# Local attention in windows of 64: transfers of 512 rows instead of 256, four q and k rows per partition, and small extra loads

## The chip, the core and the metric

The kernel runs on one NeuronCore of a Trainium2 chip. The metric is the device time of one execution, in microseconds, and lower is better. A profile shows one execution; its span is about 1.9 us shorter than the device time.

Three words are used throughout. A *transfer* is one DMA instruction. It is cut into *packets*, each on one of the core's 16 *DMA engines*. An engine that has finished its share of a transfer reports it, so each transfer has 16 *landings* (the records of the kernel before hold 4,240 for 265 transfers), and it is complete at the last.

## The reference, cut to what matters

```python
B, S, D, W = 4, 4096, 1536, 64          # q, k, v: float32, 16,384 rows of 1,536
logits = einsum('bnwd,bnud->bnwu', q_w, k_w) * D**-0.5    # windows of 64 rows
attn   = exp(logits - max); attn = attn / attn.sum(-1)
out    = einsum('bnwu,bnud->bnwd', attn, v_w)
```

Each row of q, k and v is read once and each row of the output is written once. Nothing is shared between windows.

## The kernel before

The 16,384 rows are cut into 63 units of 256 rows (R = 2 rows per partition) and 2 last units of 128 rows. Loads convert float32 to fp16 on the way and are issued by Pool, three units ahead. Stores are issued by Pool too; only the three stores of the last unit come from SP.

```python
AHEAD = 3
inp  = tile_pool(bufs=AHEAD + 1)      # q, k, v: [128, 2, 1536] fp16
outp = tile_pool(bufs=4)              # output:  [128, 2, 1536] fp32
def dram(x, u):                       # two adjacent rows per partition
    return x[u.row0 : u.row0 + u.rows].rearrange("(p r) d -> p (r d)", p=P, r=u.R)

def transpose(src, xt, c0, copy):     # PE transposes into PSUM, then one copy to SBUF
    ...
    copy(out=xt[:, c0 : c0 + CG, :R, :], in_=tp)          # contiguous
def scores(u): ...                    # q, k transposed; k q^T; exp into a block-diagonal tile
def values(u, et, last):
    u.o = outp.tile([P, RM, D], FP32)                     # waits for a free output buffer
    ...                               # et^T v, scaled by 1/sum, by ScalarE and VectorE in turn
    if last: nc.sync.dma_start(...)   # three 128x512 stores

for i, u in enumerate(units):
    if i + AHEAD < N: load_all(units[i + AHEAD])          # 3 transfers
    et = scores(u); values(u, et, i == N - 1)
    if i == N - 8: ...                # this one store is cut into four transfers
    elif i < N - 1: store(u)          # 1 transfer
```

The softmax here doesn't subtract the row's maximum and nothing guards it: scores larger than these inputs give would overflow.

## Time and profile before

| | before |
|---|---|
| device time | 953.67 us (952.92 to 954.0, 3 runs) |
| HBM traffic | 302 MB read, 101 MB written |
| DMA, mean share of the span | full in 39 of 40 slices |
| PE, DVE, ACT busy | 66%, 38%, 31% |
| last landing, end of span | 950.8 us, 952.2 us |

These are lines of the page of the kernel before. The DMA row holds the busy share of the 16 engines in 40 slices of the span, in tenths, with 9 for 90% or more. The queue lines hold packets, MB, and packet time as a share of 16 engines' span. The COPY lines hold the count, the busy time and the mean ns of one copy, and then the engine's idle time before it.

```profile
span 952.2 us, 13234 instructions
...
PE 629.0 (66%) x5624; PEld 430.1 (45%) x5624; DVE 363.6 (38%) x584; ACT 291.0 (31%) x515; POOL 139.8 (15%) x267
...
DMA  9999999999999999999999999999999999999997
...
DMA packets 37868, 252.53 MB, mean 265 GB/s; under 512 B 4264, under 2 KB 4264, under 8 KB 29752
...
q0 software_dynamic: 37376, 250.89, 101.9%
q8 instruction: 44, 0.72, 0.3%
...
L131 DVE COPY xk<-tp 128x1024 f16<-128x1024 f16 (+1 forms) x128 | 88.2, 689 | 253.4 <-PE tp L130 253.4
...
L131 ACT COPY xk<-tp 128x1024 f16<-128x1024 f16 (+1 forms) x65 | 65.4, 1006 | 354.3 <-PE tp L130 354.3
```

The DMA engines are full from start to end and no compute engine is. The list of waits says the same from the other side. Its columns are the waiting engine and line, what it waited for, total us, times, and the longest wait:

```profile
engine line waited for: us in total, times, longest us
...
POOL k L82 <- DMA k<-in_k_dram: 180.3, 58, 4.0
...
PE tp L130 <- DMA k<-in_k_dram: 127.1, 63, 3.0
...
PE tp L130 <- DMA q<-in_q_dram: 59.6, 48, 8.1
```

PE waits for loads. Pool waits as well: it issues a transfer every 3.66 us, a transfer lands 28.8 us after its issue, so about eight are under way, and Pool issues the next only when an older one is done.

The packet records add the price of a packet. Packets that carry 12,288 bytes of HBM traffic start 455 ns apart on one engine, and packets of 6,144 bytes 229 ns apart. Twice the bytes cost 226 ns more, so about 3 ns belong to the packet itself; 6,144 bytes in 226 ns are 27.2 bytes per ns and engine. (To a tenth, from the distances of packets one to four places apart on an engine: 229.3 and 455.2 ns, and 907.0 ns for the packets of 24,576 bytes of the changed kernel. Either doubling leaves 3.4 ns for the packet, so the 3.5 ns used below agrees with the trace.) It is the HBM side that counts here: a load writes only 6,144 bytes of fp16 into SBUF, a store reads 12,288 bytes from it, and yet their packets are spaced alike, 455 and 456 ns. The 474 ns that the trace records for one load packet are no measure of its price, as a packet overlaps the next.

### The profile page before, as it was taken

The numbers are of one execution on the slowest core, as the hardware profiler recorded it, in microseconds if no ns is written. First come the engines' busy times: TensorE is split into PE (matmuls) and PEld (weight loads), VectorE is DVE, ScalarE is ACT, GpSimd is POOL, SyncE is SP. The second block draws the span as 40 slices with busy tenths as digits, with TensorE's granted clock in tenths as the row PEclk, the third lists the DMA queues.
The fourth block names the chain that finished last, engine by engine and source line by source line (L and its number), as shares of the span: only waits on it lengthen the run. The fifth ranks groups of instructions, "written<-read, shape, count | busy, mean of one in ns | idle before, by whom it ended". The sixth has DMA issues, their size and how long they took to land. (4 is left out here: it accounts for less than half of the span.)

```text
span 952.2 us, 13234 instructions
## 1 busy us (share of the span) xinstructions
PE 629.0 (66%) x5624; PEld 430.1 (45%) x5624; DVE 363.6 (38%) x584; ACT 291.0 (31%) x515; POOL 139.8 (15%) x267
## 2 busy tenths in 40 slices
PE   5766666676757666766666676756766667667663
PEld 3544344454445444444444454444443445444442
DVE  3434434334343342433433334334333343443432
ACT  2432332323323233233232323322323233233232
POOL 3111111111111111111111111111111111111210
PEclk9989998989998998999999889899999898999896
DMA  9999999999999999999999999999999999999997
GB/s 185 209 280 274 255 281 255 273 277 251 281 267 262 280 254 275 273 257 281 263 266 279 256 275 268 261 281 262 267 273 262 275 265 263 277 265 268 270 279 263
DMA packets 37868, 252.53 MB, mean 265 GB/s; under 512 B 4264, under 2 KB 4264, under 8 KB 29752
## 3 DMA queue, kind: packets, MB, share of 16 engines
q0 software_dynamic: 37376, 250.89, 101.9%
q8 instruction: 44, 0.72, 0.3%
q1 hardware_dynamic: 432, 0.79, 0.2%
q14 instruction: 16, 0.13, 0.0%
HBM read 301.99 MB, written 100.66 MB: 423 GB/s over the span
## 5 line engine op out<-in xcount | busy, mean ns | idle before, releaser
L136 PE MATMUL lt<-xq,xk 128*128 128x256 f16 (+1 forms) x1536 | 228.9, 305 | 19.8 <-DVE xk L131 19.4
L130 PE MATMUL tp<-ident,k 128*128 128x128 f16 x1536 | 132.1, 247 | 128.1 <-DMA k<-in_k_dram 127.1
L136 PEld LDWEIGHTS <-xk 128*128 128x128 f16 x1536 | 154.8, 109 | 69.3 <-DVE xk L131 40.9
L131 DVE COPY xk<-tp 128x1024 f16<-128x1024 f16 (+1 forms) x128 | 88.2, 689 | 253.4 <-PE tp L130 253.4
L180 PE MATMUL o<-v,et 128*128 128x512 f16 x762 | 184.2, 378 | 0.0
L130 PEld LDWEIGHTS <-k 128*128 128x128 f16 x1536 | 113.8, 113 | 144.6 <-DMA k<-in_k_dram 139.3
L131 ACT COPY xk<-tp 128x1024 f16<-128x1024 f16 (+1 forms) x65 | 65.4, 1006 | 354.3 <-PE tp L130 354.3
L188 DVE TENSOR_SCALAR out_sb<-o,rs 128x512 f32<-128x512 f32 x191 | 143.4, 751 | 69.0 <-PE o L180 68.9
L186 ACT ACTIVATE out_sb<-o,rs 128x512 f32<-128x512 f32 x193 | 132.6, 688 | 82.6 <-PE o L180 82.5
L159 ACT ACTIVATE et<-lt,zeros 32x128 f16<-32x128 f32 (+1 forms) x256 | 91.7, 358 | 215.7 <-PE lt L136 210.9
L131 DVE COPY xq<-tp 128x1024 f16<-128x1024 f16 (+1 forms) x193 | 121.4, 681 | 54.1 <-PE tp L130 53.2
L130 PE MATMUL tp<-ident,q 128*128 128x128 f16 x1536 | 100.7, 224 | 60.1 <-DMA q<-in_q_dram 59.6
L130 PEld LDWEIGHTS <-q 128*128 128x128 f16 x1536 | 89.5, 100 | 89.8 <-DMA q<-in_q_dram 88.6
L180 PEld LDWEIGHTS <-et 128*128 128x128 f16 x762 | 68.7, 96 | 84.4 <-issue 24.2
L173 DVE RECIPROCAL rs<-sp 128x2 f32<-128x2 f32 (+1 forms) x65 | 11.1, 171 | 203.0 <-PE sp L168 203.0
L168 PE MATMUL sp<-ones,et 128*128 128x1 f16 x254 | 16.2, 167 | 106.5 <-ACT et L159 106.5
L168 PEld LDWEIGHTS <-et 128*128 128x128 f16 x254 | 10.6, 96 | 124.5 <-ACT et L159 124.5
L196 POOL DMA_DIRECT2D out_dram<-out_sb x65 | 34.9, 537 | 210.7 <-ACT et L159 103.9
L82 POOL DMA_DIRECT2D v<-in_v_dram x65 | 34.5, 531 | 199.0 <-DMA v<-in_v_dram 123.0
L82 POOL DMA_DIRECT2D q<-in_q_dram x65 | 34.7, 534 | 189.1 <-DMA q<-in_q_dram 145.3
L82 POOL DMA_DIRECT2D k<-in_k_dram x65 | 34.5, 531 | 189.6 <-DMA k<-in_k_dram 180.3
L207 POOL DMA_DIRECT2D out_dram<-out_sb x2 | 1.0, 510 | 6.3 <-ACT et L159 3.2
(10 smaller groups left out, 3.0 us busy)
## 6 DMA issues: line engine op xcount, KB each, us to landing
out_dram<-out_sb POOLq DMA_DIRECT2D x62, 1536.0 KB, 28.7
q<-in_q_dram POOLq DMA_DIRECT2D x63, 768.0 KB, 28.8
k<-in_k_dram POOLq DMA_DIRECT2D x63, 768.0 KB, 28.8
v<-in_v_dram POOLq DMA_DIRECT2D x63, 768.0 KB, 28.8
out_dram<-out_sb POOLq DMA_DIRECT2D x1, 1344.0 KB, 19.0
q<-in_q_dram POOLq DMA_DIRECT2D x2, 384.0 KB, 24.2
k<-in_k_dram POOLq DMA_DIRECT2D x2, 384.0 KB, 22.4
v<-in_v_dram POOLq DMA_DIRECT2D x2, 384.0 KB, 20.6
```

Of the source, the lines that this page charges most:

```text
L82: nc.gpsimd.dma_start(out=dst, in_=dram(src, u))
L130: nc.tensor.transpose(tp[:, c - c0, r, :], src[:, r, c * P : (c + 1) * P], ident)
L131: copy(out=xt[:, c0 : c0 + CG, :R, :], in_=tp)
L136: nc.tensor.matmul(lv[:, r, :, :], lhsT=xk[:, c, r, :], rhs=xq[:, c, :R, :], start=(c == 0 and r == 0), stop=(c == DC - 1), skip_group_che ...
L159: nc.scalar.activation(et[s, :, :, s], lv[s, :, :, s], EXP, bias=zeros[s], scale=scale)
L168: nc.tensor.matmul(sp[:, t, 0:1], lhsT=et[:, r, t, :], rhs=ones[:, 0:1], start=(r == 0), stop=(r == R - 1),)
L173: nc.vector.reciprocal(out=rs, in_=sp[:, :, 0])
L180: nc.tensor.matmul(o, lhsT=et[:, r, t, :], rhs=u.v[:, r, sl], start=(r == 0), stop=(r == R - 1),)
L186: nc.scalar.activation(dst, o, COPY, bias=0.0, scale=rs[:, t : t + 1])
L188: nc.vector.tensor_scalar_mul(dst, o, scalar1=rs[:, t : t + 1])
L196: nc.gpsimd.dma_start(out=dram(of, u)[a:b], in_=src[a:b])
L207: nc.gpsimd.dma_start(out=dst[:, r, :], in_=src[:, r, :])
```

## The change

The intent is to pay less per byte moved. A unit becomes 512 rows, so there are half as many transfers. q and k take four adjacent rows per partition, so their packets double to 24,576 HBM bytes. v and the output stay at two rows per partition. The attention blocks are still 256 rows, so the transposed q and k have to be re-interleaved in the copy out of PSUM. The memory for that comes from fewer buffers: two output buffers of 512 rows stand for four of 256. Two PSUM pools change as well: `lt_ps` goes from one buffer to two, `o_ps` from three to two. Fourteen tiny loads of 1 to 15 rows that nobody uses are added from unit 13 to unit 27 of 32, apparently to shift work between DMA engines, and the cut of one late store goes.

```diff
-AHEAD = 3
+AHEAD = 2
+SLOTS = 4
...
+    units = [Unit(i * UR, [(0, 4, 2)]) for i in range(N - 1)]          # UR = 512
+    units.append(Unit((N - 1) * UR, [(0, 2, 2), (2, 3, 1), (3, 4, 1)]))
...
-    xtp = ctx.enter_context(tc.tile_pool(name="xtp", bufs=2))
-    outp = ctx.enter_context(tc.tile_pool(name="outp", bufs=4))
+    xtp = ctx.enter_context(tc.tile_pool(name="xtp", bufs=1))
+    outp = ctx.enter_context(tc.tile_pool(name="outp", bufs=2))
...
+        r = R if name == "v" else hi - lo
+        dst = slots(getattr(u, name), lo, hi, r)
+        nc.gpsimd.dma_start(out=dst, in_=rows(src, u.first[i], hi - lo, r))
...
-            copy(out=xt[:, c0 : c0 + CG, :R, :], in_=tp)
+            dst = xt[:, c0 : c0 + CG, :].rearrange("p c (r e j) -> p (c r) j e", r=R, j=H)
+            copy(out=dst, in_=tp)
...
-        if i == N - 8:
-            ...                                   # one store cut into four transfers
+        n = ui - 12
+        if 1 <= n <= 15 and n != 8:
+            w = 128 + 4 * n
+            nc.gpsimd.dma_start(out=probe[:n, n, :w], in_=qf[0:n, :w])
```

ScalarE also takes 5 of 12 copies instead of 2 of 12.

More of the change, by code (lines that the diff above doesn't have):

```diff
@@ L17, with __init__ @@
 class Unit:
-    def __init__(self, row0, R):
-        self.row0, self.R = row0, R
-        self.rows = P * R
-def plan(total):
-    tail = [1, 1]
-    units, row = [], 0
-    body = total - P * sum(tail)
-    while row < body:
-        units.append(Unit(row, 2))
-        row += units[-1].rows
-    for R in tail:
-        units.append(Unit(row, R))
-        row += units[-1].rows
-    assert row == total
-    return units
-AHEAD = 3
+    def __init__(self, row0, parts):
+        self.row0, self.parts = row0, parts
+        self.first = [row0 + P * lo for lo, hi, R in parts]
+AHEAD = 2
+SLOTS = 4
 @with_exitstack
@@ L56 @@
     scale = float(D) ** -0.5
-    RM = 2
     qf, kf, vf, of = (x.rearrange("b s d -> (b s) d") for x in (q, k, v, out))
-    units = plan(B * S)
-    N = len(units)
+    UR = P * SLOTS
+    N = B * S // UR
+    units = [Unit(i * UR, [(0, 4, 2)]) for i in range(N - 1)]
+    units.append(Unit((N - 1) * UR, [(0, 2, 2), (2, 3, 1), (3, 4, 1)]))
     consts = ctx.enter_context(tc.tile_pool(name="consts", bufs=1))
     inp = ctx.enter_context(tc.tile_pool(name="inp", bufs=AHEAD + 1))
-    xtp = ctx.enter_context(tc.tile_pool(name="xtp", bufs=2))
@@ L66 @@
-    outp = ctx.enter_context(tc.tile_pool(name="outp", bufs=4))
+    xtp = ctx.enter_context(tc.tile_pool(name="xtp", bufs=1))
+    outp = ctx.enter_context(tc.tile_pool(name="outp", bufs=2))
     rsp = ctx.enter_context(tc.tile_pool(name="rsp", bufs=4))
     tp_ps = ctx.enter_context(tc.tile_pool(name="tp_ps", bufs=3, space=bass.MemoryType.PSUM))
-    lt_ps = ctx.enter_context(tc.tile_pool(name="lt_ps", bufs=1, space=bass.MemoryType.PSUM))
-    o_ps = ctx.enter_context(tc.tile_pool(name="o_ps", bufs=3, space=bass.MemoryType.PSUM))
+    lt_ps = ctx.enter_context(tc.tile_pool(name="lt_ps", bufs=2, space=bass.MemoryType.PSUM))
@@ L71, with rows, slots @@
+    o_ps = ctx.enter_context(tc.tile_pool(name="o_ps", bufs=2, space=bass.MemoryType.PSUM))
     s_ps = ctx.enter_context(tc.tile_pool(name="s_ps", bufs=1, space=bass.MemoryType.PSUM))
-    def dram(x, u):
-        return x[u.row0 : u.row0 + u.rows].rearrange("(p r) d -> p (r d)", p=P, r=u.R)
     ctx.enter_context(tc.manual_schedule())
-    def load(u, name):
+    def rows(x, row0, n, r):
+        return x[row0 : row0 + P * n].rearrange("(h p r) d -> p h (r d)", p=P, r=r)
+    def slots(t, lo, hi, r):
+        return t[:, lo:hi, :].rearrange("p (h r) d -> p h (r d)", r=r)
@@ L79, in load @@
+    def load(u, i, name):
+        lo, hi, R = u.parts[i]
+        if not hasattr(u, name):
+            setattr(u, name, inp.tile([P, SLOTS, D], FP16, tag=name + "16", name=name + "16"))
         src = {"q": qf, "k": kf, "v": vf}[name]
-        t = inp.tile([P, RM, D], FP16, tag=name + "16", name=name + "16")
-        dst = t[:, : u.R, :].rearrange("p r d -> p (r d)")
-        nc.gpsimd.dma_start(out=dst, in_=dram(src, u))
-        setattr(u, name, t)
+        r = R if name == "v" else hi - lo
+        dst = slots(getattr(u, name), lo, hi, r)
+        nc.gpsimd.dma_start(out=dst, in_=rows(src, u.first[i], hi - lo, r))
@@ L85, in load_all @@
     def load_all(u):
-        for name in "qkv":
-            load(u, name)
+        for i in range(len(u.parts)):
+            for name in "qkv":
+                load(u, i, name)
     load_all(units[0])
@@ L108 @@
     ets = {}
-    for R in sorted({u.R for u in units}):
+    for R in (2, 1):
         ets[R] = []
@@ L115, with scores, product @@
     turn = {R: 0 for R in ets}
-    def scores(u):
-        R = u.R
-        CG = 4 if R == 2 else 6
-        xq = xtp.tile([P, DC, RM, P], FP16, tag="xq", name="xq")
-        xk = xtp.tile([P, DC, RM, P], FP16, tag="xk", name="xk")
-        lt = lt_ps.tile([P, 512], FP32, tag="lt", name="lt")
-        lv = lt[:, : R * R * P].rearrange("p (r s e) -> p r s e", r=R, s=R)
+    flip = [0]
+    def scores(u, i):
+        lo, hi, R = u.parts[i]
+        n = hi - lo
+        H = n // R
+        CG = {4: 2, 2: 4, 1: 6}[n]
+        xq = xtp.tile([P, DC, n * P], FP16, tag="xq", name="xq")
+        xk = xtp.tile([P, DC, n * P], FP16, tag="xk", name="xk")
+        lts = []
+        for h in range(H):
+            lt = lt_ps.tile([P, 512], FP32, tag="lt", name="lt")
+            lts.append(lt[:, : R * R * P].rearrange("p (r s e) -> p r s e", r=R, s=R))
         def transpose(src, xt, c0, copy):
-            tp = tp_ps.tile([P, CG, R, P], FP16, tag="tp", name="tp")
+            tp = tp_ps.tile([P, CG * R, H, P], FP16, tag="tp", name="tp")
             for c in range(c0, c0 + CG):
                 for r in range(R):
-                    nc.tensor.transpose(tp[:, c - c0, r, :], src[:, r, c * P : (c + 1) * P], ident)
-            copy(out=xt[:, c0 : c0 + CG, :R, :], in_=tp)
-        def product(c0):
+                    for j in range(H):
+                        nc.tensor.transpose(
+                            tp[:, (c - c0) * R + r, j, :],
+                            src[:, lo + R * j + r, c * P : (c + 1) * P],
+                            ident,
+                        )
+            dst = xt[:, c0 : c0 + CG, :].rearrange("p c (r e j) -> p (c r) j e", r=R, j=H)
+            copy(out=dst, in_=tp)
+        def product(c0, h):
             for c in range(c0, c0 + CG):
+                kc = xk[:, c, :].rearrange("p (r h e) -> p r h e", r=R, h=H)
+                qc = xq[:, c, :].rearrange("p (r h e) -> p r h e", r=R, h=H)
                 for r in range(R):
                     nc.tensor.matmul(
-                        lv[:, r, :, :],
-                        lhsT=xk[:, c, r, :],
-                        rhs=xq[:, c, :R, :],
+                        lts[h][:, r, :, :],
+                        lhsT=kc[:, r, h, :],
+                        rhs=qc[:, :, h, :],
                         start=(c == 0 and r == 0),
@@ L146, in scores, with values @@
         for c0 in starts:
-            transpose(u.q, xq, c0, nc.vector.tensor_copy)
-        for i, c0 in enumerate(starts):
-            transpose(u.k, xk, c0, nc.scalar.copy if i == 1 else nc.vector.tensor_copy)
-            if i > 0:
-                product(starts[i - 1])
-        product(starts[-1])
-        et = ets[R][turn[R] % 2]
-        turn[R] += 1
-        n = W // R
-        for w in range(P // n):
-            s = slice(w * n, (w + 1) * n)
-            nc.scalar.activation(et[s, :, :, s], lv[s, :, :, s], EXP, bias=zeros[s], scale=scale)
-        return et
-    def values(u, et, last):
-        R = u.R
-        u.o = outp.tile([P, RM, D], FP32, tag="out_sb", name="out_sb")
+            flip[0] += 1
+            transpose(getattr(u, "q"), xq, c0, nc.scalar.copy if flip[0] % 3 == 0 else nc.vector.tensor_copy)
+        for g, c0 in enumerate(starts):
+            transpose(getattr(u, "k"), xk, c0, nc.scalar.copy if g % 2 == 1 else nc.vector.tensor_copy)
+            if g > 0:
+                for h in range(H):
+                    product(starts[g - 1], h)
+        blocks = []
+        for h in range(H):
+            product(starts[-1], h)
+            et = ets[R][turn[R] % 2]
+            turn[R] += 1
+            w = W // R
+            for a in range(0, P, w):
+                s = slice(a, a + w)
+                nc.scalar.activation(
+                    et[s, :, :, s], lts[h][s, :, :, s], EXP, bias=zeros[s], scale=scale
+                )
+            blocks.append((h, et))
+        return blocks
+    def values(u, i, h, et, last):
+        lo, hi, R = u.parts[i]
+        if not hasattr(u, "o"):
+            u.o = outp.tile([P, SLOTS, D], FP32, tag="out_sb", name="out_sb")
         sp = s_ps.tile([P, R, 2], FP32, tag="sp", name="sp")
@@ L180, in values @@
                     nc.tensor.matmul(
-                        o, lhsT=et[:, r, t, :], rhs=u.v[:, r, sl],
+                        o, lhsT=et[:, r, t, :], rhs=u.v[:, lo + R * h + r, sl],
                         start=(r == 0), stop=(r == R - 1),
                     )
-                dst = u.o[:, t, sl]
+                dst = u.o[:, lo + R * h + t, sl]
                 if n % 2 == 0:
@@ L190, in values, with store @@
                 if last:
-                    nc.sync.dma_start(out=of[u.row0 : u.row0 + u.rows, sl], in_=u.o[:, 0, sl])
-    def store(u, parts=((0, P),)):
-        src = u.o[:, : u.R, :].rearrange("p r d -> p (r d)")
-        for a, b in parts:
-            nc.gpsimd.dma_start(out=dram(of, u)[a:b], in_=src[a:b])
-    for i, u in enumerate(units):
-        if i + AHEAD < N:
-            load_all(units[i + AHEAD])
-        et = scores(u)
-        values(u, et, i == N - 1)
-        if i == N - 8:
-            src = u.o[0:8, : u.R, :]
-            dst = of[u.row0 : u.row0 + 8 * u.R].rearrange("(p r) d -> p r d", r=u.R)
-            for r in range(u.R):
-                nc.gpsimd.dma_start(out=dst[:, r, :], in_=src[:, r, :])
-            store(u, ((8, 16), (16, P)))
-        elif i < N - 1:
-            store(u)
+                    nc.sync.dma_start(out=of[u.first[i] : u.first[i] + P, sl], in_=dst)
+    def store(u, i):
+        lo, hi, R = u.parts[i]
+        nc.gpsimd.dma_start(out=rows(of, u.first[i], hi - lo, R), in_=slots(u.o, lo, hi, R))
+    probe = consts.tile([16, 16, 192], FP32, name="probe")
+    for ui, u in enumerate(units):
+        if ui + AHEAD < N:
+            load_all(units[ui + AHEAD])
+        n = ui - 12
+        if 1 <= n <= 15 and n != 8:
+            w = 128 + 4 * n
+            nc.gpsimd.dma_start(out=probe[:n, n, :w], in_=qf[0:n, :w])
+        for i in range(len(u.parts)):
+            last = ui == N - 1 and i == len(u.parts) - 1
+            for h, et in scores(u, i):
+                values(u, i, h, et, last)
+            if not last:
+                store(u, i)
 _INS = ['q', 'k', 'v']
```

## The prediction

> **What bounds it now: the DMA engines' data rate.** The slice table shows DMA at 9 tenths in all but the last slice; the queue table has the software queue at 101.9% of 16 engines. PE is busy 66%, DVE 38%, ACT 31%. In the list of waits PE waits for k (127 us) and q (60 us), and the Pool timeline shows one transfer issued every 3.66 us, each blocked until an older one lands: the queue is never empty. In the packet records, packets of 12,288 HBM bytes follow each other on one engine at 455 ns, those of 6,144 at 229 ns: a packet by itself costs 3 ns. The recorded 474 ns of a load packet overlaps its successor. [...] The floor: 402.65 MB are 2,048 such packets per engine, 932 us, before start, completion packets and imbalance.
>
> **The imbalance.** The 16 completion times of one transfer spread from 0.8 us at first to 9 us at the end. 44 instruction-fetch packets (16 KB, 0.9 us each) recur with period 8: eight engines carry 5 or 6 each and end 5.5 to 9 us behind. The slowest sets the end.
>
> **What the change does.**
> - q and k: one packet of 24,576 HBM bytes instead of two of 12,288; per 512 rows 16 fewer packets per engine, 16 x 3.5 ns = 0.06 us.
> - Transfers per 512 rows halve from 8 to 4. A fast engine takes 14.63 us per 256 rows; its 32 packets explain 14.56, so a boundary costs 18 ns; 4 fewer: 0.07 us. A transfer's latency (28.8 us, nearly all queueing) is already hidden.
> - Together 0.13 us of 29.28 us per 512 rows, times 31: 4 us. The removed split of one late store: 0.2 us.
> - 14 tiny loads: a completion packet per engine and few short packets, 0.4 us. They can't move work between engines, as large transfers give each engine eight partitions anyway. PE's instruction count is unchanged (11,250), so fetches and lag stay.
> - Compute: interleaved writes make DVE copies slower (0.69 to about 1.1 us, an estimate[...]); ACT takes 5 of 12 copies instead of 2. Now a unit ends 10.3 us after k lands (PE timeline); I estimate 19 us for 512 rows, 11 us after v lands. The period is 29 us and 30 us of transfers stand behind it: DMA never starves, slower copies cost nothing.
> - Tail: the last loads are followed by 20 us of stores, into which the last compute fits. Start: unchanged.
>
> **Prediction: 949.8 us, 80% range 944.5 to 954.5.** Faster by over 2% (below 935): 3%; within 2%: 94%; slower: 3%. More than 2% would have to beat the floor plus start and lag.
>
> **What would show it.** Right: DMA at 9 tenths throughout; about 29.15 us per 512 rows; q and k packets of 12,288 written bytes spaced 907 ns; final lag 8 to 10 us; DVE copies near 1.1 us without effect. Wrong: packets split again (952); a shrinking spread of landings (tiny loads do balance: up to 4 us more, as the mean lag is 4 and the slowest 9); DMA slices below 9[...].
>
> **What would make it wrong.** Long packets that delay fetches or run at another rate per byte; compute outlasting the stores at the end; tiny loads stalling an engine for their latency; contention from engines moving to other partitions.

## More of the kernel before

Times here are medians.

## The result, and the profile after

| | before | after |
|---|---|---|
| device time | 953.81 us (4 runs) | 954.15 us (953.58 to 955.36, 4 runs) |
| ratio, 95% interval | | 1.0007 [0.999, 1.0024] |
| packets in the software queue | 37,376 | 27,824 |
| DVE copy, ACT copy | 0.69, 1.01 us | 1.27, 1.29 us |
| last landing, end of span | 950.8, 952.2 us | 950.9, 951.8 us |

A ratio is the mean time of one kernel's runs over that of the other's of the same rounds, so it is not quite the ratio of the medians.

The gain of 4 us that was forecast is absent. These are the lines of the page of the changed kernel that answer to those above:

```profile
span 951.8 us, 12993 instructions
...
PE 668.1 (70%) x5624; PEld 439.5 (46%) x5624; DVE 424.8 (45%) x489; ACT 431.0 (45%) x610; POOL 91.6 (10%) x154
...
DMA  9999999999999999999999999999999999999996
...
DMA packets 28313, 252.57 MB, mean 265 GB/s; under 512 B 2545, under 2 KB 2656, under 8 KB 12256
...
q0 software_dynamic: 27824, 250.96, 100.6%
q8 instruction: 44, 0.72, 0.3%
...
L141 ACT COPY xk<-tp 128x1024 f16<-128x1024 f16 (+1 forms) x96 | 123.5, 1287 | 233.8 <-PE tp L135 233.8
...
L141 DVE COPY xk<-tp 128x1024 f16<-128x1024 f16 (+1 forms) x97 | 123.3, 1271 | 178.6 <-PE tp L135 178.6
```

The packets did get fewer, and those of q and k start 907 ns apart, as forecast. The body of the kernel did get faster too. The landings of the transfers give the time per 512 rows, taken over 24 units in the middle and averaged over the 16 engines. It is 29.406 us before; with the changed kernel it is 29.289 us, taken from the run without the tiny loads below, where equal stretches are easily counted (29.307 us with them). The difference of 0.117 us, times 31, is 3.6 us.

So the gain is earned in the body and lost elsewhere. The page's slices are 24 us wide and hide the place; shorter stretches show it. These lines of the stretch view hold, for each stretch, its length, the busy time of each engine with its instructions, the granted PE clock, the DMA share and GB/s. GB/s counts bytes as they are written, so a load, which turns float32 into fp16, counts half of its HBM traffic. This is the kernel before:

```profile
100.00:840.00 740.00, 495.32 (x4420) 338.37 (x4420) 284.94 (x452) 225.97 (x401) 106.75 (x201) 0.92 1.03 268
...
920.00:936.00 16.00, 10.12 (x86) 6.52 (x84) 5.43 (x10) 6.18 (x12) 2.14 (x4) 0.93 1.05 309
936.00:950.00 14.00, 6.04 (x40) 3.81 (x40) 2.59 (x5) 2.79 (x5) 0.00 (x0) 0.50 0.69 274
```

And these are the same stretches of the changed kernel:

```profile
100.00:840.00 740.00, 534.33 (x4462) 350.77 (x4458) 337.01 (x377) 339.23 (x477) 70.02 (x114) 0.88 1.02 270
...
920.00:936.00 16.00, 3.47 (x8) 1.05 (x8) 1.50 (x2) 2.01 (x3) 0.00 (x0) 0.52 0.90 358
936.00:950.00 14.00, 7.76 (x81) 5.45 (x79) 5.24 (x10) 6.32 (x12) 1.09 (x2) 0.87 0.59 237
```

From 920 to 936 us PE of the changed kernel does 8 matmuls instead of 86, and Pool issues nothing. From 936 to 950 us the DMA engines have too little to do, at 237 GB/s. The list of waits of the changed kernel for 905 to 952 us names the cause:

```profile
engine line waited for: us in total, times, longest us
POOL out_dram L214 <- DVE xq L141: 23.1, 1, 23.1
...
ACT out_sb L205 <- DMA out_dram<-out_sb: 14.1, 1, 14.1
DVE out_sb L207 <- DMA out_dram<-out_sb: 13.6, 1, 13.6
```

Pool's wait is put down to a DVE copy, but that is only the last semaphore of several; the first place to look is ScalarE. This is its timeline in the changed kernel (start, us, what, and in brackets the idle time before it and what ended it):

```profile
916.19 1.51 ACT L174 ACTIVATE et<-lt,zeros 32x128 f16<-32x128 f32 x4 [2.58 <-PE lt L148]
931.79 0.69 ACT L205 ACTIVATE out_sb<-o,rs 128x512 f32<-128x512 f32 x1 [14.09 <-DMA out_dram<-out_sb]
```

The last unit has its scores at 917.7 us, but it may not write its output: with two output buffers it needs the one of the unit two before, and the store of that unit, issued at 910.1 us, has landed completely only at 931.7 us, as it stood in a deep queue. After that, three small blocks of compute are left, each with its store. The queue runs dry meanwhile: the last store that was waiting in it ends on the 16 engines between 931.0 and 939.0 us, and the next one is issued at 937.6 and lands at 942.9 us.

### The profile page after: what moved, and what is told of

Its sections match the earlier page's. It is cut to its first block, busy times and chain, and to the rows that moved or that the text cites. A ratio compares the mean times of both kernels' runs of the same rounds, so it can differ in the third digit from the quotient of the medians.

```text
span 951.8 us, 12993 instructions
## 1 busy us (share of the span) xinstructions
PE 668.1 (70%) x5624; PEld 439.5 (46%) x5624; DVE 424.8 (45%) x489; ACT 431.0 (45%) x610; POOL 91.6 (10%) x154
## 3 DMA queue, kind: packets, MB, share of 16 engines
q0 software_dynamic: 27824, 250.96, 100.6%
## 4 chain that ended last, share of the span: by engine, by line
DMA 63%; PE 13%; ACT 7%; another core or an unknown queue 7%; DVE 6%; issue 2%; POOL 1%; ACTq 0%; POOLq 0%; DVEq 0%
DMA out_dram<-out_sb 47%; DMA q<-in_q_dram 9%; PE o L199 8%; DMA k<-in_k_dram 7%; PE lt L148 3%; ACT out_sb L205 3%; DVE out_sb L207 3%; PE tp L135 3%; ACT et L174 2%; ACT xk L141 2%; DVE xk L141 2%; DVE xq L141 1%; ACT xq L141 0%; POOL out_dram L214 0%
## 5 line engine op out<-in xcount | busy, mean ns | idle before, releaser
L199 PE MATMUL o<-v,et 128*128 128x512 f16 x762 | 237.6, 420 | 91.2 <-ACT out_sb L205 86.8
L141 ACT COPY xk<-tp 128x1024 f16<-128x1024 f16 (+1 forms) x96 | 123.5, 1287 | 233.8 <-PE tp L135 233.8
L141 DVE COPY xk<-tp 128x1024 f16<-128x1024 f16 (+1 forms) x97 | 123.3, 1271 | 178.6 <-PE tp L135 178.6
L199 PEld LDWEIGHTS <-et 128*128 128x128 f16 x762 | 74.0, 101 | 220.3 <-issue 183.3
L141 DVE COPY xq<-tp 128x1024 f16<-128x1024 f16 (+1 forms) x129 | 152.2, 1255 | 12.6 <-PE tp L135 12.5
L141 ACT COPY xq<-tp 128x1024 f16<-128x1024 f16 x64 | 82.1, 1283 | 91.4 <-PE tp L135 91.4
L214 POOL DMA_DIRECT2D out_dram<-out_sb x33 | 23.8, 720 | 391.2 <-DVE out_sb L207 269.9
L187 PEld LDWEIGHTS <-et 128*128 128x128 f16 x254 | 14.3, 102 | 61.8 <-ACT et L174 50.3
L79 POOL DMA_DIRECT2D v<-in_v_dram x34 | 23.6, 694 | 180.8 <-DMA out_dram<-out_sb 51.1
L79 POOL DMA_DIRECT2D q<-in_q_dram x34 | 18.6, 546 | 114.1 <-DMA probe<-in_q_dram 53.1
L79 POOL DMA_DIRECT2D k<-in_k_dram x34 | 18.6, 547 | 78.2 <-DMA k<-in_k_dram 37.2
```

The costliest lines, as they stand in the source:

```text
L79: nc.gpsimd.dma_start(out=dst, in_=rows(src, u.first[i], hi - lo, r))
L141: copy(out=dst, in_=tp)
L187: nc.tensor.matmul(sp[:, t, 0:1], lhsT=et[:, r, t, :], rhs=ones[:, 0:1], start=(r == 0), stop=(r == R - 1),)
L199: nc.tensor.matmul(o, lhsT=et[:, r, t, :], rhs=u.v[:, lo + R * h + r, sl], start=(r == 0), stop=(r == R - 1),)
L214: nc.gpsimd.dma_start(out=rows(of, u.first[i], hi - lo, R), in_=slots(u.o, lo, hi, R))
```

## The experiments

Runs sent together share a chip and the runs of the kernel before. Unless said otherwise each had five rounds, and the kernel before has 9 runs in each group.

### The changed kernel again

> The changed kernel again, as the yardstick of this chip. Every theory expects what was measured: the same time as the kernel before, ratio 0.999 to 1.002.

Measured: 953.95 us against 952.86 us, ratio 1.001 [0.9997, 1.0022]. The absence of a gain stands.

### Without the tiny loads

```diff
-        n = ui - 12
-        if 1 <= n <= 15 and n != 8:
-            ...
-            nc.gpsimd.dma_start(out=probe[:n, n, :w], in_=qf[0:n, :w])
```

> The changed kernel without its 14 tiny loads. My prediction: they cost 0.4 us and balance nothing, so 0 to 0.6 us faster than the changed kernel, and the spread of the 16 landings at the last 512-row store stays near 8 us. Rival (the tiny loads balance the DMA engines): 2 us or more slower, and the spread grows. Rival (each tiny load stalls an engine for its latency, and that ate the gain): 4 us faster.

Measured: 953.23 us, ratio to before 1.0001 [0.9987, 1.0014], 0.7 us below the changed kernel of the same chip. The interval of each ratio is wider than that difference, but all five runs (952.45 to 953.61 us) lie below all five of the changed kernel (953.70 to 954.56 us), so it is a small cost. The spread of the 16 landings of the last 512-row store is 7.8 us without them and 8.5 us with them in this group (8.0 us in the first profile of the changed kernel). They balance nothing, and they are not where 4 us went.

### With a third output buffer

The tiny loads and their tile of 12 KB per partition are left out to make room for the third output buffer. So this run is to be read against the one before it.

```diff
-    outp = ctx.enter_context(tc.tile_pool(name="outp", bufs=2))
+    outp = ctx.enter_context(tc.tile_pool(name="outp", bufs=3))     # and no tiny loads
```

> No tiny loads (that frees the memory) and three output buffers of 512 rows instead of two. Theory (the last unit cannot write its output before the store of the unit two before it has landed, so the queue runs dry at the end): the 14 us wait of ScalarE for a store near the end is gone, the queue stays full to the end, and the time falls by 4 to 5 us against the run without tiny loads, to about 949 us, ratio to the kernel before 0.995. Rival (the gain was never there, or the slower PSUM copies ate it): within 1 us of the run without tiny loads.

Measured: 951.9 us, ratio to before 0.9988 [0.9975, 1.0001]; 1.3 us below the run without tiny loads, not 4 to 5. In the trace the mechanism came out fully. The two late stretches of this run, in the same columns as above:

```profile
920.00:936.00 16.00, 8.82 (x88) 5.22 (x86) 5.90 (x12) 7.64 (x13) 1.09 (x2) 0.97 1.02 413
936.00:950.00 14.00, 0.00 (x0) 0.00 (x0) 0.00 (x0) 0.00 (x0) 0.00 (x0) 0.50 0.43 175
```

The wait is gone from ScalarE's timeline:

```profile
916.65 1.51 ACT L174 ACTIVATE et<-lt,zeros 32x128 f16<-32x128 f32 x4 [2.58 <-PE lt L148]
918.96 0.69 ACT L205 ACTIVATE out_sb<-o,rs 128x512 f32<-128x512 f32 x1 [0.80 <-PE o L199]
```

All compute is over before 936 us, DMA stays full to there, and the last landing comes at 946.8 us, against 950.5 us without the third buffer and 950.8 us in the kernel before. That is about the 4 us that the prediction promised, at the last landing. (The 3.7 us compare two runs of one chip. The profile of the kernel before is of an execution of 954.1 us, up to 1.3 us longer than that kernel's medians in the other groups, so the 4.0 us against it may hold as much too much.) But the span ends at 950.0 us, 3.2 us after it, where in the kernel before it ended 1.5 us after. The semaphore records show who was late: SP had seen its last store at 946.9 us, and Pool came to the closing barrier only at 949.3 us. Pool spends that time in the drain instruction at the end of the program.

These are end times in us after the start of the span, taken from the records of the runs (those further down included). "Pool" and "SP" are the last landing of a transfer issued by each:

```
                                 Pool    SP      Pool's drain ends   span ends
before                           949.4   950.8   951.5               952.2
changed                          947.0   950.9   950.0               951.8
no tiny loads                    946.3   950.5   948.9               951.4
third output buffer              946.6   946.8   949.2               950.0
  and last unit stored from SP   945.8   946.9   948.3               949.1
    same, two rows per partition 947.2   948.1   948.3               949.1
  and last two units from SP     945.2   947.0   947.7               948.5
  and last three units from SP   944.5   949.0   947.0               950.0
```

In each row the drain ends later than Pool's last landing, by 2.1 to 3.0 us in all but one and by 1.2 us in that one. In the changed kernel SP's last landing is later than the drain, and in the kernel before the drain outlasts it by 0.7 us only. The drain does not wait for all data, whoever issued it: in the changed kernel and in the last row it ends before SP's last landing. The third buffer brings SP's landing forward to Pool's, and the drain comes out as the last thing to end, 2.4 us after the data.

### The kernel before with two output buffers

```diff
-    outp = ctx.enter_context(tc.tile_pool(name="outp", bufs=4))
+    outp = ctx.enter_context(tc.tile_pool(name="outp", bufs=2))     # of 256 rows
```

> The kernel before with two output buffers of 256 rows instead of four. Theory of the output buffers: its last block too has to wait for a late store, so 2 to 4 us slower than the kernel before, all of it in the last 30 us, with the period per 512 rows still 29.3 us. Rival (output buffers do not matter, as compute has idle time): within 0.5 us of the kernel before.

Measured: 954.32 us, ratio 1.0014 [1.0002, 1.0027]: slower, by 1.5 us and so less than expected. The waits of this run (columns as above) show how little a wait tells by itself:

```profile
engine line waited for: us in total, times, longest us
ACT out_sb L186 <- DMA out_dram<-out_sb: 231.8, 61, 14.1
DVE out_sb L188 <- DMA out_dram<-out_sb: 201.1, 61, 13.6
```

ScalarE now waits for a store in 61 of the 65 units, 232 us in all, a line that the kernel before does not have at all. Yet the time per 512 rows is 29.404 us against 29.406. The waits cost nothing in the body, where the queue holds work for longer than they last. So the loss lies outside the body. In the profile the last landing comes at 951.3 us instead of 950.8, and the 16 landings of the last stores lie within 0.3 us, so there too the queue had run dry. The rest of the 1.5 us is not traced.

### The end, with the last unit stored from SP

```diff
+        queue = nc.sync if u is units[-1] else nc.gpsimd
-        nc.gpsimd.dma_start(out=rows(...), in_=slots(...))
+        queue.dma_start(out=rows(...), in_=slots(...))      # on top of the third buffer, no tiny loads
```

> Three output buffers, no tiny loads, and the two stores of the last unit that Pool issued are now issued from SP, so that Pool's last transfer lands some 7 us earlier. Theory (in the run with three buffers the data was done at 946.8 us but Pool reached the closing barrier only at 949.3 us, 2.7 us after its last transfer had landed; that delay ate the gain): Pool is no longer last, the span ends about 0.9 us after the last landing, near 947.7 us, and the time is 949.0 to 950.2 us, ratio to the kernel before 0.9966. Rival (the end is set by something else): as with Pool stores, 951.9 us, ratio 0.9988.

Measured: 950.79 us against 953.69 us, ratio 0.9973 [0.9961, 0.9986]. The drain theory was right in direction, but gained only about two thirds of what was expected from it (the ratio went from 0.9988 to 0.9973, where 0.9966 was expected): Pool's last transfer did not land 7 us earlier but at 945.8 us. SP's stores shared the engines with it and passed it: SP's store that was issued after Pool's last one had landed by 935.6 us, and Pool's landed by 945.8 us; from 926 to 934 us, 129 large packets of SP's queue started beside 150 of Pool's. (Together that is one per 459 ns on each of 16 engines, about the spacing of one queue alone.)

### Two rows per partition for q and k as well

This run moves the same 512 rows per transfer, but with the packets of the kernel before and contiguous copies.

```diff
-        r = R if name == "v" else hi - lo
+        r = R
-            dst = xt[:, c0 : c0 + CG, :].rearrange("p c (r e j) -> p (c r) j e", r=R, j=H)
+            dst = xt[:, c0 : c0 + CG, :].rearrange("p c (r j e) -> p (c r) j e", r=R, j=H)
```

> As the run with SP stores at the end, but q and k are loaded with two adjacent rows per partition, as v is: twice the packets for q and k, the same number of transfers, and contiguous PSUM copies. My prediction of 3.5 ns per packet: 0.06 us more per 512 rows, so 1.7 to 1.9 us slower than that run. Rival (packet size is worth nothing): equal within 0.5 us. Rival (the interleaved copies cost time): faster by 1 us or more.

Measured: 950.74 us, ratio to before 0.9971 [0.9959, 0.9984], equal to the run above, so the expectation for the time failed. In the body the expected cost is there: 29.345 us per 512 rows against 29.283 us, 0.05 to 0.06 us more by whichever transfer one follows, where 0.056 were forecast. The last landing is at 948.1 us instead of 946.9. In both runs, though, Pool's drain ended at 948.3 us, and it set the end in both (here only 1.2 us after Pool's last landing, which hides the later data; why, no run shows, so the equal times are a coincidence as far as is known). The run splits the gain of the change: of 0.12 us per 512 rows, half comes from the longer packets and half from fewer transfers. Both are as small as the 3.5 ns per packet and 18 ns per transfer of the prediction.

### The changed kernel with contiguous copies, wrong on purpose

```diff
-            dst = xt[:, c0 : c0 + CG, :].rearrange("p c (r e j) -> p (c r) j e", r=R, j=H)
+            dst = xt[:, c0 : c0 + CG, :].rearrange("p c (r j e) -> p (c r) j e", r=R, j=H)
```

The rows are then paired wrongly, and the result is wrong. This run had three rounds (4 runs).

> The changed kernel with contiguous instead of interleaved PSUM copies: rows are paired wrongly, so the result is wrong on purpose. Theory (the copies are off the path, the end waits for an output buffer): DVE copies back near 0.69 us and ScalarE copies near 1.0 us, but the time equals the changed kernel's within 0.5 us, about 954. Rival (slower copies ate the gain): 2 to 4 us faster.

Measured: 953.96 us, ratio to before 1.0007 [0.9991, 1.0022], the time of the changed kernel. Two lines of its page show that the copies did become fast:

```profile
L141 ACT COPY xk<-tp 128x1024 f16<-128x1024 f16 (+1 forms) x96 | 96.7, 1008 | 235.7 <-PE tp L135 235.7
...
L141 DVE COPY xk<-tp 128x1024 f16<-128x1024 f16 (+1 forms) x97 | 66.8, 689 | 237.4 <-PE tp L135 237.4
```

Summed over the q and k copies of both engines, the copies of the changed kernel are busy for 481 us (123.5 + 123.3 + 152.2 + 82.1) and those of this run for 311 us (96.7 + 66.8 + 82.8 + 64.5). The 170 us of additional work on two engines cost no time. The slower copies are not where the gain went.

### The kernel before with late stores from SP

```diff
+        queue = nc.sync if u in units[-3:] else nc.gpsimd
```

> The kernel before with the stores of its third- and second-last blocks issued from SP. Theory of Pool's late close: there Pool was last too, reaching the barrier at 951.5 us, 2.1 us after its last transfer landed at 949.4, against 950.9 for SP; so 0.5 to 0.9 us faster than before, no more, as the slowest DMA engine's work is the same. Rival (stores from SP are cheaper in themselves): 2 us or more faster.

Measured: 954.01 us, ratio 1.0009 [0.9996, 1.0021]. It did not get faster, so this expectation failed too. The trace shows why: SP's stores share the engines with the loads of the last unit, which stand in Pool's queue. The last load landed at 944.9 us instead of 939.7, the last unit was computed later, and SP's last store landed at 952.2 us instead of 950.8. Stores from SP are no cheaper; they only go to another place in the line.

### Two units stored from SP

```diff
-        queue = nc.sync if u is units[-1] else nc.gpsimd
+        queue = nc.sync if u in units[-2:] else nc.gpsimd
```

> As the run with SP stores at the end, but the store of the second-last 512-row unit is issued from SP as well. In that run Pool's last transfer (that very store) was overtaken by SP's and landed only at 945.8 us, and Pool's closing drain ended at 948.3 us. Theory (the drain ends 1 to 3 us after Pool's last transfer has landed): Pool's last transfer now lands before 942 us, its drain ends before 945, SP is last, the span ends 0.9 us after the last landing, near 947.8 us, and the time is 949.2 to 950.0 us, 1 us below the run before it. Rival (the drain ends when all data has been moved, whoever issued it): no change, 950.8 us.

Measured: 950.04 us against 953.18 us, ratio 0.9968 [0.9954, 0.9981]. The time is at the edge of what was expected, but the way there was not: Pool's last transfer landed at 945.2 us, not before 942, and its drain still ended last, at 947.7 us. This is the fastest version, and it beats both kernels by a third of a per cent. Its lead over the run with one unit (ratio 0.9973 [0.9961, 0.9986]) is within the noise.

### Uneven stores, to even out the engines

The tiny loads had one use: their packets have sizes of their own, so the trace shows on which engines a transfer of n partitions lands. Their start times fit one reading, that n partitions go to the same first n engines, the first four of which are early ones: from two rows on a load of n rows has n packets, and from 9 to 15 rows the first four start within 0.94 us in each load (0, 0.11, 0.46 and 0.94 us), while the rows added start later, the last of the 15 at 7.98 us.

```diff
+        cuts = [0, 112, 116, 120, 124, P] if u in units[-3:-1] else [0, P]
+        for a, b in zip(cuts, cuts[1:]):
+            queue.dma_start(out=dst[a:b], in_=src[a:b])
```

> As the run with two units stored from SP, but the 512-row stores of the third-last and second-last units are cut: 112 partitions go out evenly, and the last 16 in four transfers of four partitions each. The tiny loads of the changed kernel showed that a transfer of n partitions uses the same first n engines, and that the first four are among those without instruction fetches. Theory (lag comes from the fetches, and only an uneven split can even it out): the first four engines get 5.5 us more work, the others 1.8 us less, the spread of the last landings falls from about 8.7 us to 7 or less, and the time falls by 1.5 to 1.8 us against the run of this call without the cuts. Rival (lag is not a matter of work per engine, or the small transfers cost more than they shift): no gain, or slower.

Measured: 957.58 us, ratio 1.0045 [1.0032, 1.0059], slower by 7.5 us than the run without the cuts. The large late packets grew: 35 of those after 880 us took over 1.2 us, and none in the run without cuts.

```diff
-        cuts = [0, 112, 116, 120, 124, P] ...
+        cuts = [slice(0, 112)] + [slice(112 + a, P, 4) for a in range(4)] ...
```

> As the run with the cut stores, but each of the four-partition transfers takes every fourth of the last 16 partitions instead of four adjacent ones. There, 46 of the late large packets took over 1.2 us; in the run without cuts none did. Theory[...]: the packets over 1.2 us go down to 10 or fewer, and the time falls from 957.6 us to 949 to 952 us. Rival (the partition order does not matter; any such cut costs this much): again about 957 us.

(The 46 in this text were counted with a limit of 1.0 us; with 1.2 us it is 35.) Measured: 954.55 us, ratio 1.0008 [0.9995, 1.0022], and 15 packets over 1.2 us. Spreading the partitions took back 3 us of the 7.5 and 20 of the 35 long packets, so the order of the partitions matters. Why it does was not shown. And about half of the loss remained, and neither theory's number was met. Whether the lag of eight engines can be evened out at all is left open.

### Three units stored from SP

```diff
-        queue = nc.sync if u in units[-2:] else nc.gpsimd
+        queue = nc.sync if u in units[-3:] else nc.gpsimd
```

> As the run with two units stored from SP, but three. Theory (Pool's closing drain ends 1 to 3 us after its last transfer, and SP's transfers share the engines with Pool's): Pool's last transfer is now a load and lands before 940 us, its drain ends before 943, SP is last and the span ends 0.9 us after the last landing: 949.2 to 950.0 us, 0 to 0.8 us below the run with two units. Rival (as in the kernel before with SP stores: the loads are pushed back, and the last blocks are computed too late): 950.5 us or more.

Measured: 952.58 us, ratio 0.9993 [0.9981, 1.0006]. The rival was right: the last load landed at 944.5 us, the last output was computed at 946.8 us, and SP's last store landed at 949.0 us. So two units are better than three; from one unit they can't be told apart.

## Why the prediction was wrong

**Right: the bound.** The DMA engines' byte rate is the limit (their share is 1.03 and 1.02 from 100 to 840 us, before and after), and the floor of 932 us was not approached. Slower copies, more ScalarE work and, in the run with two output buffers, 232 us of new ScalarE waits all left the body at the same time per 512 rows.

**Right: the size of the gain in the body.** 0.13 us per 512 rows were forecast and 0.117 us measured. (The 29.28 and 29.15 us of the prediction are those of a fast engine; the earliest of the 16 went from 29.28 to 29.17 us.) The two terms were tested apart: longer packets 0.06 us (0.06 forecast), fewer transfers the rest, 0.06 us (0.07 forecast). With the third buffer, the last landing is 4.0 us earlier than in the kernel before (946.8 against 950.8 us), of which 0.2 us were forecast from the store that is no longer cut.

**Right: the tiny loads.** They move nothing; removing them gained 0.7 us, where 0.4 us had been forecast; the 0.3 us between are within the noise of the runs.

**Right in effect, off in size: the copies.** VectorE's went from 0.69 to 1.27 us, not 1.1, which was the author's estimate. The interleaved write, with a step of two elements, is what made them slower: with contiguous writes and nothing else changed, in the run that was wrong on purpose, they took 0.69 us again. That ScalarE's copies would slow down as well, from 1.01 to 1.29 us, was not foreseen. Neither cost time.

**Wrong: the tail.** The step that failed is this one: "Tail: the last loads are followed by 20 us of stores, into which the last compute fits." The count of stores was right. The compute would have fit, as the run with a third buffer shows, where all of it was over before 936 us. What was overlooked is that compute needs a place to write. The prediction costed packets, transfers and copies, but passed over one line of the diff, four output buffers becoming two. They hold the same bytes, so it looked neutral. But a buffer is released only when the whole store from it has landed, so what counts is how late in the queue that store lands. In both kernels it is the store of 1,024 rows earlier, four units back before and two units back after. But with larger transfers a store takes 44.0 us from issue to landing instead of 28.7 us. Before, it had landed 14 to 18 us ahead of the unit's first output write in the body, and 8 to 9 us ahead in the last two units. After, ScalarE's first output write of a unit follows that landing by 0.1 to 1.0 us in nearly every unit, the last one included; with a third buffer 28 to 31 us lie between, and 16 us in the last unit. In the body this costs nothing. In the last unit it held compute for 14 us, emptied the queue, and put the last landing at 950.5 us (950.9 us with the tiny loads) instead of the 946.8 of the run with three buffers. The warning "compute outlasting the stores at the end" stood in the prediction, but with no number and no cause.

**Wrong in part: how the end follows the last landing.** The prediction took the end of the program to stay at the same distance from the last landing. It does not: Pool's drain ends 1.2 to 3.0 us after Pool's last transfer, and all but 0.7 us of that was covered in the kernel before by SP's stores. That is why the third buffer brought the last landing forward by 3.7 us but the time by only 1.3 us, and why the two runs that stored late units from SP got part of the rest.

**The account of the time.** From the kernel before, the body takes off 3.6 us. The wait for the output buffer gives 3.7 us back at the last landing (946.8 us with three buffers, 950.5 us with two). The tiny loads add some 0.5 us to that (950.9 us in the changed kernel, where the kernel before has 950.8 us). The end of the span follows by 1.5 us before and 0.9 us after, and the device times are equal within the noise. The landings come from one profile each, so sums of this kind are good to about 1 us.

**Open.** What Pool's drain does in these 1.2 to 3.0 us, and what sets their number. Whether the lag of the late engines comes from the instruction fetches, as the prediction says: the period of eight and the steps of about 1 us fit (there are 44 packets of 16 KB, of 0.88 to 0.98 us each, and the 16 landings of the late stores spread by 8 to 9 us), but no run took the fetches away. Why the uneven stores cost as much as they did. What the other changed lines do by themselves (loads 1,024 rows ahead instead of 768, the PSUM pools, one `xtp` buffer instead of two): no run took them back one by one, though with a third output buffer the gain at the last landing is as forecast without them.

## What to carry to other kernels

When a kernel is limited by DMA, price a change per packet and per transfer from the spacing of packets in the trace, not from the recorded duration of a packet or the latency of a transfer: here halving the transfers and doubling packets that were already large was worth 0.4%. When buffers get larger and fewer, ask at the last iterations which store must have landed before the last tile may be written, since a wait that is free while the queue is deep costs time where nothing stands behind it (here a wait of 14 us cost 3.7 us at the last landing). And look at which engine reaches the end of the program last: an engine that issued a transfer may stay busy for some time after the data has landed (here 1.2 to 3.0 us).
